# A two-block transformer kernel: tile sizes rounded to 64 bytes, and a pool mixer that leaves PSUM in one VectorE instruction

## The chip, the cores and the metric

The kernel runs on one core of a Trainium2 chip, in fp32. The metric is the device time of one execution in microseconds (us), as the median of three runs.

## The reference, cut to what matters

A first block of two attention layers gives x. It ends in a normalisation by `final_norm_gain`. A second block of one layer follows: a pooling mixer on the normalised x, added to x, and then a convolutional feed-forward network (FFN), added again. All sequences are 1024 long and 1024 wide.

```python
def pool_mixer(x, w, b, scale):              # x: normalised once more
    cs = jnp.pad(jnp.cumsum(xf, axis=1), ((0, 0), (1, 0), (0, 0)))
    for gi, w_len in enumerate((2, 4, 8, 16)):          # four groups of 256 features
        c = cs[..., gi * 256:(gi + 1) * 256]
        lo = jnp.maximum(pos + 1 - w_len, 0)
        window_sum = c[:, 1:] - jnp.take(c, lo, axis=1)
        groups.append(window_sum / count - xf[..., gi * 256:(gi + 1) * 256])
    d = jnp.stack(groups, axis=2)
    y = jnp.einsum('bsgc,gcd->bsgd', d, w).reshape(bsz, seq, 1024) + b
    return scale * y

def conv_ffn(x, w_in, conv_w, conv_b, w_out):           # hidden 2816, conv of 3 taps
    val, gate = jnp.split(causal_depthwise_conv(x @ w_in, conv_w, conv_b), 2, axis=-1)
    return (jax.nn.silu(gate) * val) @ w_out

x = x + pool_mixer(rms_norm(x, norm_mix_g), pool_w, pool_b, pool_scale)
x = x + conv_ffn(rms_norm(x, norm_ffn_g), ffn_w_in, ffn_conv_w, ffn_conv_b, ffn_w_out)
```

## The kernel before

Activations lie feature by feature: 128 features of a tile on the partitions, 512 tokens (a "chunk" c) along the free dimension. A projection in full precision is three matmuls of 128x512 on rounded halves (`mm3`, L257, L260, L261): high weights by high activations, high by low, low by high. For each weight tile `load_w` takes a DMA into a buffer `wraw` (three buffers), a ScalarE rounding into `whi` (L238) and a subtraction into `wlo` (L138) on VectorE or GpSimd. All DMAs are issued from the SyncE queue, in order. The order of the instructions on each engine is drawn up ahead by a scheduler that simulates the program and goes by priorities; on the chip every engine runs its own list in order and waits on semaphores.

The stages that the change touches come last:

- `out1` projects the outputs of the second attention layer with `wo1`. Its operands are eight tiles in `hh`/`hl` and the tiles `yh8` to `yl11` of `y_parts` (eight tiles of 4096 bytes a partition), from a pool allotted at the right-hand end of the memory; a pool `oj` there holds the residual `xr`. Layer 0's projection uses `y_parts` too, but from a pool on the left.
- `pool_chunk(c)` is the normalisation and the mixer of one chunk, once for each half of the tokens. For each of eight feature tiles k it forms the twice normalised activation `h` in VectorE (L1403), scales x in place to the residual (ScalarE by `gf`, L1404, then GpSimd by `bf`, L1405), adds shifted copies for the window sum (L1413), and forms the difference `df` (L1417, L1419, L138). `dense32` then loads the group's weights through the ring `wraw` (`load_f32`), multiplies in fp32 (L313, two instructions per pair of tiles) and leaves PSUM by ScalarE with scale and bias into a tile `pt` (L1429); VectorE adds `pt` to x (L1430), and `norm_split` rounds the result to `hh` (L1178) and `hl` (L1179) for the FFN and sums its squares on GpSimd (L1190).
- Chunk 0 of the mixer is woven with `out1`'s projection of chunk 1; chunk 1 of the mixer is woven with the first six FFN feature tiles of chunk 0 (`FC`).
- `ffn` then alternates blocks of input projections (operands `hh`/`hl`) with blocks of output projections (operands `ah`/`al`, ten tiles of 4096 bytes from the pool `ff`). A convolution buffer `hz` and its carry `ht` come first in that pool.

Tiles of a pool are allotted back to back, each rounded up to 32 bytes a partition. In the program before this gives the following start addresses, by the remainder of a division by 64 bytes. `vecs` (968 bytes, 992 allotted) puts `onesr`, `two` and `bd` at a remainder of 32, and `bd` (8 bytes, 32 allotted) brings the pools behind it back to 0: weights, `hh`, `hl`, `ev`, and nearly all tiles of both attention layers. The right-hand end at which the pools of `out1` begin, counting down, is 229344, a remainder of 32; all tiles of `y_parts` and `xr` there stand at 32. In `ff`, `ht` (352 bytes) puts one of the two `hz` and all of `ah` and `al` at 32.

Of the kernel before, what the change touches and what calls it, by code (L numbers as in the profile page):

```python
# [8 lines left out]
F32 = mybir.dt.float32  # L9
F32R = mybir.dt.float32r  # L10
AF = mybir.ActivationFunctionType
ALU = mybir.AluOpType
# [21 lines left out]
NVEC = _vec_layout()  # L34

GORD = (0, 1, 3, 2)
# [104 lines left out]
class Build:  # L141
# [57 lines left out]
    def setup(self):  # L199
        nc = self.nc  # L200
        c = self.const = self.pool("const", 1)
        self.ident = c.tile([128, 128], F32, name="ident")
        self.dma(out=self.ident, in_=self.A["ident"])
        self.vecs = c.tile([128, NVEC], F32, name="vecs")
        self.dma(out=self.vecs, in_=self.A["vecs"])
        self.onesr = c.tile([128, 128], F32R, name="onesr")
        self.ones = raw(self.onesr)
        nc.gpsimd.memset(self.ones, 1.0)
        two = c.tile([128, 256], F32R, name="two")
        nc.gpsimd.memset(raw(two), 0.0)  # L210
        nc.gpsimd.memset(raw(two[:, 64:192]), 2.0)
        self.twor = two[:, 64:192]
        self.sel = [two[:, 128:256], two[:, 0:128]]
        self.bd = c.tile([128, 2], F32, name="bd")
        nc.gpsimd.memset(self.bd, 0.0)
        nc.gpsimd.memset(self.bd[0:64, 0:1], 1.0)
        nc.gpsimd.memset(self.bd[64:128, 1:2], 1.0)
        self.small = self.pool("small", 2)
        self.wp = self.pool("wp", 4)
        self.mm = self.pool("mm", 2, PSUM)  # L220
# [6 lines left out]
    def load_w(self, src, n, engs=None):  # L227

        nc = self.nc
        res = []  # L230
        for o in range(0, n, 512):
# [3 lines left out]
            for q in range(0, m, 512):  # L235
# [5 lines left out]
                res += [(hi[:, i:i + 128], lo[:, i:i + 128], hi, lo) for i in range(0, e, 128)]  # L241
        return res

    def load_f32(self, src, n):

        res = []
        for o in range(0, n, 512):
            m = min(512, n - o)
            w = self.wp.tile([128, m], F32, tag="wraw", name="w", bufs=self.wp.bufs - 1)
            self.dma(out=w, in_=src[:, o:o + m])  # L250
            res += [w[:, i:i + 128] for i in range(0, m, 128)]
        return res
# [25 lines left out]
    def dense(self, src, rhs, nk, evac, chunks=(0, 1), cw=512, key=None, ps_pool=None, ks=None, engs=None):  # L278
# [26 lines left out]
        return Job(lambda: self.load_w(src, nk * 128, engs), body, key, getattr(self, "done", None))  # L305

    def dense32(self, src, rhs, nk, evac, chunks=(0, 1), ps_pool=None):

        def body(w):
            for c in chunks:  # L310
                ps = (ps_pool or self.mm).tile([128, 512], F32, tag="mm", name="ps")
                for k in range(nk):
                    self.nc.tensor.matmul(ps, w[k], rhs(k, c), start=k == 0, stop=k == nk - 1, skip_group_check=True)  # L313
                self.run_deferred()
                evac(c, ps)
                yield 0.65 * nk
        return Job(lambda: self.load_f32(src, nk * 128), body)

# [997 lines left out]
    def out1(self):  # L1316
# [3 lines left out]
        with ExitStack() as st:  # L1320
            P = lambda n, b, **k: st.enter_context(self.tc.tile_pool(name=n + "n", bufs=b, side="right", **k))
            yp = P("yp", 1)
            oj = P("oj", 2)
# [45 lines left out]
    def pool_chunk(self, c, accf, accm, gfm, psb, invc, tail):  # L1369
# [23 lines left out]
        accz = self.rbc[:, cs]  # L1393
        keep = []
        for g in GORD:
            ds = []
            for kk in range(2):
# [5 lines left out]
                nc.vector.scalar_tensor_tensor(out=h[:, 16:528], in0=x, scalar=gfm[:, k:k + 1], in1=bm, op0=ALU.mult, op1=ALU.mult)  # L1403
                nc.scalar.activation(x, x, AF.Copy, scale=self.v("gf", k))  # L1404
                nc.gpsimd.tensor_tensor(out=x, in0=x, in1=bf, op=ALU.mult)  # L1405
                if c == 0:
                    nc.gpsimd.tensor_copy(tail[:, k, :], h[:, 512:528])
# [14 lines left out]
                yield 1.0  # L1422
            for f in range(2):
                ft = 2 * g + f

                def evac(_, ps, ft=ft):
                    x = X[:, ft, cs]
                    t = oj.tile([128, 512], F32, tag="df", name="pt", bufs=2)
                    nc.scalar.activation(t, ps, AF.Identity, scale=self.v("ps", ft), bias=psb[:, ft:ft + 1])  # L1429
                    nc.vector.tensor_tensor(out=x, in0=x, in1=t, op=ALU.add)  # L1430
                    self.norm_split(x, "gz", ft, self.hh[:, ft, cs], self.hl[:, ft, cs], accz, ft == 2 * GORD[0], keep if ft in GK[7:] else None)
                yield from self.dense32(A["wpl"][ft], lambda k, c: ds[k], 2, evac, (c,), ps_pool=self.px)
        rz = self.rstd([accz] + keep, 4, f"rz{c}", px)
# [4 lines left out]
    def ffn(self, before):  # L1438
# [6 lines left out]
        with ExitStack() as st:  # L1445
            f = st.enter_context(self.tc.tile_pool(name="ff", bufs=2))
            ht = f.tile([128, 44, 2], F32, name="ht", bufs=1)
            nc.gpsimd.memset(ht, 0.0)
# [3 lines left out]
            def conv_evac(j, i, kind):  # L1452
                def evac(c, ps):
                    cs = slice(c * 512, (c + 1) * 512)
                    z = f.tile([128, 514], F32, tag="hz", name="hz", bufs=2)
                    nc.vector.tensor_copy(z[:, 0:2], ht[:, j, :])
# [205 lines left out]
```

## Time and profile before

| | |
|---|---|
| median of 3 runs | 2449.55 us (2443.07 to 2453.1) |
| profiled execution | 2446.46 us, span 2444.7 us |
| mean granted TensorE clock | 0.977 |
| TensorE matmul busy | 2333.7 us, 95% of the span |
| VectorE, ScalarE, GpSimd busy | 1729.5, 1088.9, 925.1 us |

The span runs from the first to the last instruction of the profiled execution. A busy matmul row includes its pipelined end, so the pace of matmuls is read from how many start in a stretch. An engine's idle time counts only where something on the path to the end waits for it. `PEld` is the weight load that goes with each matmul; its count in a stretch is that of the matmuls that begin there.

### The profile page before, as it was taken

The numbers are of one execution on the slowest core, as the hardware profiler recorded it, in microseconds if no ns is written. First come the engines' busy times: TensorE is split into PE (matmuls) and PEld (weight loads), VectorE is DVE, ScalarE is ACT, GpSimd is POOL, SyncE is SP. The second block draws the span as 40 slices with busy tenths as digits, with TensorE's granted clock in tenths as the row PEclk, the third lists the DMA queues.
The fourth block names the chain that finished last, engine by engine and source line by source line (L and its number), as shares of the span: only waits on it lengthen the run. The fifth ranks groups of instructions, "written<-read, shape, count | busy, mean of one in ns | idle before, by whom it ended". The sixth has DMA issues, their size and how long they took to land.

```text
span 2444.7 us, 32782 instructions
## 1 busy us (share of the span) xinstructions
PE 2333.7 (95%) x11118; PEld 1910.1 (78%) x11118; DVE 1729.5 (71%) x2856; ACT 1088.9 (45%) x2037; POOL 925.1 (38%) x773
## 2 busy tenths in 40 slices
PE   7989999989999999999999999999899999999999
PEld 6966777767878878888888887866678888888887
DVE  6767886777895557777887889598977464646554
ACT  5425555565663445434443445444444131323231
POOL 3117887891120235646674762475600000000000
PEclk9989999999999999999999999999899999999999
DMA  6752234234456566776766656422222111111112
GB/s 206 215 147 65 77 106 134 78 108 132 128 197 208 197 198 180 193 199 177 216 170 189 182 177 230 153 88 72 63 80 80 44 52 45 51 48 48 49 47 91
DMA packets 234111, 312.74 MB, mean 128 GB/s; under 512 B 101815, under 2 KB 119671, under 8 KB 233944
## 3 DMA queue, kind: packets, MB, share of 16 engines
q1 hardware_dynamic: 233944, 310.65, 42.1%
q8 instruction: 88, 1.44, 0.2%
q14 instruction: 79, 0.65, 0.1%
HBM read 223.45 MB, written 87.03 MB: 127 GB/s over the span
## 4 chain that ended last, share of the span: by engine, by line
PE 73%; DVE 12%; DMA 4%; issue 4%; POOL 3%; ACT 2%; SPq 0%; DVEq 0%; POOLq 0%; ACTq 0%
PE ps L260 20%; PE ps L257 20%; PE ps L261 20%; DVE wlo L138 2%; PE s L550 2%; PE o L610 2%; PE s L551 2%; PE o L609 2%; POOL acc L599 1%; POOL pl L138 1%; DVE pl L138 1%; PE s L1218 1%; PE s L810 1%; DVE mcg L811 1%; PE pt L915 1%
## 5 line engine op out<-in xcount | busy, mean ns | idle before, releaser
L257 PE MATMUL ps<-hh,whi 128*128 128x512 f32 x1888 | 749.1, 399 | 18.4 <-ACT hh L411 8.5
L260 PE MATMUL ps<-hl,whi 128*128 128x512 f32 x1888 | 751.1, 398 | 8.4 <-DVE hl L412 7.6
L261 PE MATMUL ps<-hh,wlo 128*128 128x512 f32 x1888 | 751.9, 399 | 3.6 <-DVE wlo L138 2.5
L238 ACT CAST whi<-wraw 128x512 fp32r<-128x512 f32 (+1 forms) x400 | 244.9, 615 | 467.8 <-PE ps L260 375.4
L257 PEld LDWEIGHTS ps<-hh,whi 128*128 128x128 f32 x1888 | 361.7, 192 | 97.7 <-ACT hh L411 8.5
L260 PEld LDWEIGHTS ps<-hl,whi 128*128 128x128 f32 x1888 | 361.6, 192 | 87.4 <-DVE hl L412 9.3
L261 PEld LDWEIGHTS ps<-hh,wlo 128*128 128x128 f32 x1888 | 361.2, 191 | 81.7 <-DVE wlo L138 3.7
L599 POOL TENSOR_TENSOR acc<-acc,p 128x512 f32<-128x512 f32 (+2 forms) x272 | 323.8, 1198 | 238.4 <-ACT p L465 177.4
L138 DVE TENSOR_TENSOR wlo<-wraw,whi 128x512 fp32r<-128x512 f32 (+1 forms) x388 | 327.2, 847 | 73.0 <-ACT whi L238 63.9
L138 POOL TENSOR_TENSOR pl<-p,ph 128x384 fp32r<-128x384 f32 (+1 forms) x160 | 200.9, 1258 | 10.6 <-ACT ph L467 8.9
L1485 DVE TENSOR_TENSOR xacc<-ps,xacc 128x512 f32<-128x512 f32 x96 | 66.3, 691 | 131.4 <-PE ps L261 130.9
L1457 DVE TENSOR_TENSOR hz<-ps,rbc 128x512 f32<-128x512 f32 x88 | 60.6, 690 | 117.9 <-PE ps L261 114.1
L467 ACT CAST ph<-p 128x512 fp32r<-128x512 f32 (+1 forms) x240 | 131.5, 560 | 23.2 <-PE d L628 6.0
L260 PE MATMUL ps<-al,whi 128*128 128x512 f32 x352 | 139.1, 396 | 0.0
L261 PE MATMUL ps<-ah,wlo 128*128 128x512 f32 x352 | 138.7, 396 | 0.0
L257 PE MATMUL ps<-ah,whi 128*128 128x512 f32 x352 | 138.4, 396 | 0.0
L610 PE MATMUL o<-pl,V 128*64 128x512 f32 (+3 forms) x368 | 121.1, 348 | 13.8 <-POOL pl L138 7.3
L1461 ACT ACTIVATE cv<-hz,vecs 128x512 f32<-128x512 f32 x88 | 71.6, 816 | 130.7 <-DVE hz L1457 128.0
L609 PE MATMUL o<-ph,V 128*128 128x512 f32 (+3 forms) x368 | 118.6, 340 | 4.0 <-ACT ph L917 3.3
L465 ACT ACTIVATE p<-p 128x384 f32<-128x384 f32 (+2 forms) x128 | 66.6, 524 | 110.3 <-DVE p L1245 109.9
L465 ACT ACTIVATE p<-s 128x512 f32<-128x512 f32 x112 | 66.5, 596 | 80.7 <-PE s L551 47.8
L138 DVE TENSOR_TENSOR pl<-p,ph 128x512 fp32r<-128x512 f32 x80 | 85.1, 1064 | 21.7 <-ACT ph L467 19.3
(256 smaller groups left out, 4439.2 us busy)
## 6 DMA issues: line engine op xcount, KB each, us to landing
wraw<-in_w SPq DMA_DIRECT2D x116, 256.0 KB, 3.5
wraw<-in_wfi SPq DMA_DIRECT2D x112, 256.0 KB, 2.6
wraw<-in_wo SPq DMA_DIRECT2D x72, 256.0 KB, 3.1
g<-evf SPq DMA_DIRECT2D x48, 256.0 KB, 3.9
wraw<-in_wfo SPq DMA_DIRECT2D x40, 256.0 KB, 2.6
sg<-g SPq DMA_DIRECT2D x32, 256.0 KB, 2.7
y<-O SPq DMA_DIRECT2D x14, 512.0 KB
hl<-y SPq DMA_DIRECT2D x14, 512.0 KB, 9.2
```

The source lines that it names most:

```text
L138: out_eng.tensor_tensor(out=out, in0=a, in1=b, op=ALU.subtract)
L238: nc.scalar.copy(hi, raw[:, q:q + e])
L257: i = mm(ps, wh, h, start=first, stop=False, skip_group_check=True)
L260: mm(ps, wh, l, start=False, stop=False, skip_group_check=True)
L261: mm(ps, wl, h, start=False, stop=last, skip_group_check=True)
L465: nc.scalar.activation(p, s, AF.Exp)
L467: nc.scalar.copy(ph, p)
L599: nc.gpsimd.tensor_tensor(out=t, in0=t, in1=p[:, x0 - a:x1 - a], op=ALU.add)
L609: mm(o, V[s][:, j, :], P[0][:, x], start=new, stop=False, skip_group_check=True)
L610: mm(o[0:64], V[s][:, j, 0:64], P[1][:, x], start=False, stop=i == touch[g][-1], skip_group_check=True)
L1461: nc.scalar.activation(t, z[:, 2:514], AF.Identity, scale=self.v("cw2", j), bias=self.v("cb", j))
L1485: nc.vector.tensor_tensor(out=x, in0=ps, in1=x, op=ALU.add)
```

## The change

Five paddings make tile sizes multiples of 64 bytes: `vecs` from 242 to 256 columns, `bd` from 2 to 16, `ht` from 44 to 48 rows, `hz` from 514 to 528 columns, and an unused tile of 32 bytes that is allotted first at the right-hand end. With them `onesr`, `two`, `bd`, the right-hand `y_parts` and `xr`, both `hz` and all `ah` and `al` start at a remainder of 0. What is read and written in them stays as it was.

In the mixer GpSimd multiplies x by `bf` first; then one ScalarE instruction scales it by `gf` and adds the bias `psb`. PSUM is left by one VectorE instruction, x = `ps` times the mixer's scale + x; the tile `pt` and ScalarE's eviction are gone. The mixer's weights get four buffers of their own (`wpl`): four are fetched when a chunk begins, and one more behind each feature tile's matmuls. `load_f32` and `dense32` are removed.

```diff
-        self.vecs = c.tile([128, NVEC], F32, name="vecs")
+        self.vecs = c.tile([128, -(-NVEC // 16) * 16], F32, name="vecs")[:, 0:NVEC]
...
-        self.bd = c.tile([128, 2], F32, name="bd")
+        self.bd = c.tile([128, 16], F32, name="bd")[:, 0:2]
...
+            P("pad", 1).tile([128, 8], F32, name="pad")
             yp = P("yp", 1)
             oj = P("oj", 2)
...
         keep = []
+        wpl = {}
+
+        def fetch(n):
+            for i in GK[len(wpl):n]:
+                wpl[i] = oj.tile([128, 256], F32, tag="wpl", name="wpl", bufs=4)
+                self.dma(out=wpl[i], in_=A["wpl"][i])
+        fetch(4)
         for g in GORD:
...
-                nc.scalar.activation(x, x, AF.Copy, scale=self.v("gf", k))
                 nc.gpsimd.tensor_tensor(out=x, in0=x, in1=bf, op=ALU.mult)
+                nc.scalar.activation(x, x, AF.Identity, scale=self.v("gf", k), bias=psb[:, k:k + 1])
...
-            for f in range(2):
-                ft = 2 * g + f
-
-                def evac(_, ps, ft=ft):
-                    x = X[:, ft, cs]
-                    t = oj.tile([128, 512], F32, tag="df", name="pt", bufs=2)
-                    nc.scalar.activation(t, ps, AF.Identity, scale=self.v("ps", ft), bias=psb[:, ft:ft + 1])
-                    nc.vector.tensor_tensor(out=x, in0=x, in1=t, op=ALU.add)
-                    self.norm_split(x, "gz", ft, self.hh[:, ft, cs], self.hl[:, ft, cs], accz, ft == 2 * GORD[0], keep if ft in GK[7:] else None)
-                yield from self.dense32(A["wpl"][ft], lambda k, c: ds[k], 2, evac, (c,), ps_pool=self.px)
+            for ft in (2 * g, 2 * g + 1):
+                ps = self.px.tile([128, 512], F32, tag="mm", name="ps")
+                for k in range(2):
+                    nc.tensor.matmul(ps, wpl[ft][:, k * 128:(k + 1) * 128], ds[k], start=k == 0, stop=k == 1, skip_group_check=True)
+                fetch(min(len(wpl) + 1, 8))
+                x = X[:, ft, cs]
+                nc.vector.scalar_tensor_tensor(out=x, in0=ps, scalar=self.v("ps", ft), in1=x, op0=ALU.mult, op1=ALU.add)
+                self.norm_split(x, "gz", ft, self.hh[:, ft, cs], self.hl[:, ft, cs], accz, ft == 2 * GORD[0], keep if ft in GK[7:] else None)
+                yield 1.3
...
-            ht = f.tile([128, 44, 2], F32, name="ht", bufs=1)
+            ht = f.tile([128, 48, 2], F32, name="ht", bufs=1)
...
-                    z = f.tile([128, 514], F32, tag="hz", name="hz", bufs=2)
+                    z = f.tile([128, 528], F32, tag="hz", name="hz", bufs=2)
```

## Rows read from the trace of the kernel before

**Rows 1.** The page, busy us of TensorE with share and instructions.
```profile
PE 2333.7 (95%) x11118; PEld 1910.1 (78%) x11118; DVE 1729.5 (71%) x2856; ACT 1088.9 (45%) x2037; POOL 925.1 (38%) x773
```

**Rows 2.** Windows of 20 us: length, busy us (x instructions) by engine, granted clock, DMA.
```profile
1600.00:1620.00 20.00, 19.53 (x74) 13.61 (x73) 19.90 (x27) 9.92 (x16) 15.85 (x16) 1.00 0.25 75
1620.00:1640.00 20.00, 14.79 (x47) 9.70 (x46) 18.83 (x16) 9.57 (x16) 19.19 (x15) 0.83 0.34 105
...
1700.00:1720.00 20.00, 13.21 (x35) 7.43 (x34) 20.00 (x25) 9.40 (x15) 13.27 (x11) 0.80 0.19 56
...
1800.00:1820.00 20.00, 20.00 (x88) 16.17 (x87) 14.43 (x27) 5.48 (x11) 0.00 (x0) 1.00 0.21 63
```

**Rows 3.** Windows over whole FFN blocks: output, output, then input projections.
```profile
1890.41:1935.21 44.80, 44.80 (x193) 36.07 (x192) 19.07 (x29) 6.95 (x12) 0.00 (x0) 1.00 0.17 52
...
2022.28:2067.08 44.80, 44.80 (x194) 36.07 (x192) 19.07 (x29) 6.95 (x12) 0.00 (x0) 1.00 0.17 52
2067.09:2154.14 87.05, 87.05 (x385) 72.06 (x384) 54.72 (x99) 30.96 (x46) 0.00 (x0) 1.00 0.15 46
```

**Rows 4.** Windows of matmuls on y tiles alone: layer 0's, then out1's.
```profile
828.11:844.43 16.32, 16.32 (x73) 13.52 (x72) 10.71 (x13) 11.14 (x12) 2.49 (x2) 1.00 0.46 150
1548.46:1570.87 22.41, 22.41 (x97) 17.98 (x96) 14.33 (x16) 11.53 (x19) 14.54 (x12) 1.00 0.57 189
```

**Rows 5.** One line's instructions over the span: ns min/median/max, first and last start.
```profile
L628 PEld LDWEIGHTS d<-ah,two x48: 187/188/192, 251.7 to 1450.0; 128*128 128x128 f32 x48
```

**Rows 6.** Windows over the mixer's two stretches, columns as in rows 2.
```profile
1590.00:1668.00 78.00, 71.87 (x275) 51.34 (x273) 70.00 (x82) 38.05 (x63) 61.43 (x51) 0.96 0.27 85
1692.00:1783.00 91.00, 77.32 (x278) 54.36 (x276) 88.89 (x108) 45.29 (x73) 55.09 (x39) 0.91 0.22 69
```

**Rows 7.** Groups by line from 1590 to 1800: busy us, mean ns | idle before.
```profile
L1405 POOL TENSOR_TENSOR xacc<-xacc,bf 128x512 f32<-128x512 f32 x16 | 24.3, 1521 | 13.3 <-ACT xacc L1404 13.3
...
L1179 DVE SCALAR_TENSOR_TENSOR hl<-xacc,vecs,hh 128x512 fp32r<-128x512 f32 x16 | 18.9, 1184 | 1.6 <-ACT hh L1178 1.6
...
L1430 DVE TENSOR_TENSOR xacc<-xacc,pt 128x512 f32<-128x512 f32 x16 | 16.5, 1030 | 3.2 <-ACT pt L1429 3.2
...
L1429 ACT ACTIVATE pt<-ps,psb,vecs 128x512 f32<-128x512 f32 x16 | 12.2, 768 | 1.2 <-PE ps L313 1.1
...
L1404 ACT ACTIVATE xacc<-xacc,vecs 128x512 f32<-128x512 f32 x16 | 11.5, 723 | 26.9 <-DVE hx L1403 26.9
```

**Rows 8.** Single lines of VectorE: ns min/median/max; L1457 between 1590 and 1790.
```profile
L1430 DVE TENSOR_TENSOR xacc<-xacc,pt x16: 675/684/1776, 1612.3 to 1774.9; 128x512 f32<-128x512 f32 x16
...
L1457 DVE TENSOR_TENSOR hz<-ps,rbc x14: 676/679/693, 1679.4 to 1789.7; 128x512 f32<-128x512 f32 x14
```

**Rows 9.** TensorE's waits from 1590 to 1800: us in total, times, longest.
```profile
PE ps L313 <- DMA w<-in_wpl: 5.2, 2, 3.8
PE ps L257 <- DVE hz L1457: 5.0, 2, 3.6
PE ps L313 <- DVE df L1417: 4.7, 2, 2.8
PE ps L261 <- DVE wlo L138: 3.0, 3, 2.1
...
PE ps L257 <- ACT whi L238: 1.1, 2, 0.8
```

**Rows 10.** Timeline around the longest wait for mixer weights: start us, us, engine.
```profile
1622.33 0.37 SPq L158 DMA_DIRECT2D w<-in_wpl  x1
...
1624.53 0.17 DVE L138 TENSOR_TENSOR df<-df,hx 128x16 f32<-128x16 f32 x1
...
1624.92 3.75 PE L313 MATMUL ps<-df,w 128*128 128x512 f32 x4 [3.79 <-DMA w<-in_wpl]
```

**Rows 11.** Waits of the SyncE queue from 1580 to 1800, as in rows 9.
```profile
SPq L158 <- DVE wlo L138: 95.3, 32, 7.4
...
SPq L158 <- PE ps L313: 19.0, 9, 9.2
```

More of the change, by code (lines that the diff above doesn't have):

```diff
@@ L241, in load_w @@
                 res += [(hi[:, i:i + 128], lo[:, i:i + 128], hi, lo) for i in range(0, e, 128)]
[L242 to L251, printed above, removed]
         return res
@@ L305, in dense @@
         return Job(lambda: self.load_w(src, nk * 128, engs), body, key, getattr(self, "done", None))
[L307 to L317, printed above, removed]
     def held(self, srcs, rhs, nk, chunks, evacs, pools):
```

## The prediction

> **What bounds the kernel now.** I read the page first, then windows over the last third, then the waits and single lines inside the mixer. The page shows TensorE with matmuls in flight for 95% of the span [rows 1]. That share is an average over two kinds of stage. In the FFN from 1800 us on TensorE is never idle [rows 2, 3], so what a matmul costs there goes straight to the end. [...]
>
> Next I looked for whether the remainder of an address shows. It does in TensorE's pace alone. An FFN output block of 192 matmuls takes 44.80 us, 233.3 ns each, and two blocks shown agree to the last digit; an input block of 384 takes 87.05 us, 226.7 ns each [rows 3]. Form, weights and clock are the same; the moving operand is `ah`/`al` (remainder 32) in one and `hh`/`hl` (remainder 0) in the other. That could still be something else of these tiles, so the y tiles are the better witness: the same lines on the same names, first from the left pool (remainder 0) and later from the right-hand one (remainder 32). They run 72 in 16.32 us, 226.7 ns, and 96 in 22.41 us, 233.4 ns [rows 4].
>
> **The paddings.** The span holds 22 x 8 x 2 x 3 = 1056 matmuls on `ah`/`al`. Each gains 233.33 - 226.69 = 6.64 ns: 7.0 us, all of it at the bound. `out1` has 4 x 8 x 2 x 3 = 192 on the right-hand y tiles at 6.7 ns: 1.3 us, half of them in chunk 0's projection and half in the first mixer stretch. Together 8.3 us; the bounds are 0, if the remainder is not the cause, and 8.3. The weight load of `two` at remainder 32 takes a median of 188 ns [rows 5], and the load beside aligned FFN matmuls 72.06 / 384 = 188 [rows 3], so `onesr`, `two` and `bd` bring nothing. What ScalarE and VectorE write into `ah`, `al` and `hz`, and the `xr` loads, are hidden in the FFN and `out1` behind TensorE; if that cover were gone I see no row that would price them above nothing.
>
> [...]
>
> **Eviction.** Sixteen ScalarE evictions of 0.768 us leave, 12.2 us. ScalarE is half idle in both stretches (38.1 of 78, 45.3 of 91 [rows 6]); I count that at nothing. VectorE's sixteen additions L1430 stay in number and change in kind. They take 675 ns at best and 1776 at worst, 1.030 us in the mean, 16.5 us [rows 7, 8]. The delay falls on instructions with two SBUF inputs while GpSimd is at work: `hl` (L1179) stands at 1.184 in the same stretch [rows 7]. L1457 reads PSUM and one SBUF tile of the same size, in the middle of that traffic, and all fourteen lie between 676 and 693 [rows 8]. The new eviction has those operands, with a scalar from a tile besides. From below it could take 0.68 us without any delay, and if it also left GpSimd alone for as long, up to 16 x 0.684 = 10.9 us of waiting on either side would go. From above it could be delayed like L1179: 16 x 1.184 = 18.9 us, 2.4 lost. I take 0.70 by L1457, its nearest row: 11.2 us, 5.3 us less of VectorE. VectorE is full in one stretch and nearly so in the other, so I count all 5.3.
>
> [...]
>
> **Weights of their own.** TensorE waits twice for `in_wpl`, 5.2 us, once 3.8 [rows 9]. I would gladly take all of it, but the timeline shows what is late next: that load is issued at 1622.33, the matmul starts at 1624.92, and the small subtraction that finishes `df` ends at 1624.53 + 0.17 = 1624.70 [rows 10]. The weights were 0.2 us behind the data. The second wait is at most 5.2 - 3.8 = 1.4. Bounds 0 and 5.2; I take 0.2 + 1.4 = 1.6. SyncE's queue loses its waits for L313 on the ring, 19.0 us, but its large waits are for `wlo`, 95.3 us [rows 11], so the weight loads behind gain nothing while VectorE is late. The new loads 5 to 8 of a chunk, and chunk 1's first four, wait in that queue for an L313 four tiles back; the `wraw` loads of `wo1` and the FFN stand behind them. Those L313 are earlier ones than before, and the waits take the place of nine longer ones: nothing, unless the queue's order puts a fetch too early; nine such waits cost 19.0 us without showing in TensorE's list.
>
> **Residual ahead.** The order was `h`, ScalarE, GpSimd; it becomes `h`, GpSimd, ScalarE: the same two instructions in a row, 0.72 and 1.52 us [rows 7], and x is needed only after a window sum and a matmul. GpSimd stops waiting for ScalarE (13.3 us), but ScalarE, which waited for `h` (26.9 us), now also waits for GpSimd's 1.52 us. Behind it in ScalarE's list stand `whi` roundings and `hh`. Bounds: 13.3 of GpSimd's idle time gained, 16 x 1.52 = 24.3 us lost. ScalarE's slack and a list drawn up for the new order make me take 0.
>
> **The sum.** 8.3 + 5.3 + 1.6 = 15.2 us. The profiled execution took 2446.46 us, 1.8 more than its span, and would take 2431.3. The median of the runs is 3.1 above that execution, so the median to expect is **2434.4 us**, 0.6% below 2449.55.
>
> **Rivals.** *The mixer gives nothing.* VectorE and GpSimd stay as full as they are, or another order of the lists eats the 6.9 us: TensorE's other waits there, `hz` 5.0, `df` 4.7, `wlo` 3.0 [rows 9], all come from VectorE. For it: the stretch ends by VectorE, and the nearest stall moved 0.2 us. Against: the PSUM row is spared every time. Time 2449.55 - 8.3 = 2441.3.
>
> *The paddings give nothing*, since a matmul's pace goes by columns, and something else of those pools or their stages costs the 7 ns. For it: both slow families come from the last pools allotted. Against: the y tiles, and FFN blocks of the two kinds with DMA equally light (0.17 and 0.15) [rows 3]. Time 2449.55 - 6.9 = 2442.7. [...]
>
> *ScalarE stuck behind GpSimd (slower).* In program order a residual scaling that waits for GpSimd's multiplication holds up the next `whi`, then `wlo`, then the matmul and the `wraw` ring. For it: waits for `whi` already end TensorE's idle time twice (1.1 us) [rows 9], and GpSimd is at 61.4 of 78. Against: ScalarE idles for half. If every scaling is exposed by one multiplication the loss is 24.3 us and the time 2449.55 - 15.2 + 24.3 = 2458.7; if a further GpSimd instruction of that length lies ahead in each case, 48.6 us and 2483.0. Slower than before it becomes from 15.2 us, 0.95 per scaling, and measurably so from 27.5, 1.7 per scaling.
>
> **How the numbers follow.** Half a per cent, 12.2 us, is about what a measurement of this kernel can tell from no change: faster means below 2437.3, slower above 2461.8. The forecast gets 0.52; the mixer giving nothing 0.25; the paddings giving nothing 0.08; both nothing 0.03; ScalarE behind GpSimd 0.12, of which 0.05 lie above 2461.8. The forecast's own range is 2425 to 2438: downwards by the other ends, 10.9 for 5.3 and 5.2 for 1.6, upwards by the 3 us between runs. Faster: nearly all of the forecast, and 0.03 of the first rival, when it moves a little, 0.55. Slower 0.05, same 0.40. The range reaches up over the first two rivals to 2446; the third and "both nothing" are largely left out, with some of the second.
>
> **What would show it.** Right: output blocks of the FFN at 43.5 us for 192, the later y stretch at 21.8 for 96; the new eviction at 0.68 to 0.75 us in all sixteen; no wait of L313 for `wpl`; the two mixer stretches together shorter by 5 to 9 us with VectorE still full. Wrong: blocks still at 44.8 us (the remainder is not the cause); evictions at 1.1 us or more; ScalarE waiting for x of GpSimd and TensorE for `whi`; a longer stretch before 1800 in which another wait of VectorE takes over. The prediction fails upwards most easily in the mixer, whose order of instructions I can't see.

## The result, and the profile after

The changed kernel takes 2434.38 us, median of five runs (2429.21 to 2435.2), against 2449.26 for the kernel before on the same chip: 0.9941, with a 95% interval of 0.9921 to 0.9960, 14.9 us less. The forecast was 2434.4. The number was met; most of what follows says that two of its terms came out as they did for reasons other than the ones given.

The page of the changed kernel, TensorE's line, answers to [rows 1]:

```profile
PE 2319.2 (95%) x11118; PEld 1905.2 (78%) x11118; DVE 1720.1 (71%) x2856; ACT 1079.2 (44%) x2021; POOL 921.8 (38%) x773
```

The same number of matmuls keeps TensorE busy 14.5 us less. To see where, I cut both traces at two landmarks which the change leaves alone: the first matmul on the later y tiles, and the first matmul of the FFN on `ah`. Windows of the kernel before, from landmark to landmark and from there to the end (columns as in [rows 2]: length, busy us of TensorE, weight load, VectorE, ScalarE and GpSimd with instructions, granted clock, DMA share, GB/s):

```profile
1548.46:1802.70 254.24, 230.78 (x921) 172.39 (x920) 212.00 (x275) 125.81 (x207) 150.84 (x115) 0.93 0.28 88
1802.70:2444.70 642.00, 638.38 (x2785) 522.53 (x2783) 360.25 (x617) 182.68 (x273) 1.30 (x1) 1.00 0.18 57
```

The changed kernel, in order of time: the later y stretch, the window from landmark to landmark, the two mixer stretches, the window from there to the end, and an output block and an input block of the FFN ([rows 4], [rows 6], [rows 3]):

```profile
1547.28:1569.68 22.40, 22.40 (x98) 17.99 (x97) 13.38 (x16) 11.55 (x19) 14.56 (x12) 1.00 0.64 214
1547.28:1794.46 247.18, 222.98 (x921) 168.31 (x920) 201.83 (x275) 116.20 (x191) 148.91 (x115) 0.97 0.28 90
1590.00:1668.00 78.00, 71.35 (x276) 51.58 (x275) 69.10 (x85) 35.26 (x58) 63.57 (x55) 0.96 0.29 90
1692.00:1783.00 91.00, 73.44 (x281) 51.94 (x280) 88.05 (x115) 42.13 (x68) 52.09 (x38) 0.96 0.18 60
1794.46:2431.90 637.44, 633.91 (x2785) 522.45 (x2783) 360.21 (x617) 182.72 (x273) 1.29 (x1) 1.00 0.18 57
1881.78:1925.74 43.96, 43.96 (x193) 36.06 (x192) 19.07 (x29) 6.95 (x12) 0.00 (x0) 1.00 0.17 53
...
1925.74:2012.84 87.10, 87.10 (x386) 72.07 (x385) 54.72 (x99) 30.99 (x46) 0.00 (x0) 1.00 0.15 46
```

Three things are to be seen.

*The FFN* is 642.00 - 637.44 = 4.6 us shorter. An output block of 192 went from 44.80 to 43.96 us, 233.3 to 229.0 ns a matmul; 226.7 was forecast.

*The later y stretch* still takes 22.40 us for 96, 233.3 ns, although its tiles now start at a multiple of 64 bytes. The remainder, which the prediction took for the cause, is gone, and the pace has not moved.

*The mixer*, from the y stretch to the FFN, is 254.24 - 247.18 = 7.1 us shorter, where 6.9 was forecast and some of the 1.3 of the y tiles besides. But not because TensorE waits less. The same 921 matmul records are busy for 230.78 us before and 222.98 after, 7.8 us less; what is left as idle time went from 23.5 to 24.2. The granted clock rose from 0.93 to 0.97 of full speed. The times within this window at which the clock stood at its lower level, 0.50 of full speed, come to these sums, first before, then after:

```profile
sum 34.13, PE 26.73 PEld 18.43 DVE 32.26 ACT 16.22 POOL 24.07; mean PE 5.35 PEld 3.69 DVE 6.45 ACT 3.24 POOL 4.81
sum 17.07, PE 11.94 PEld 8.11 DVE 15.51 ACT 7.29 POOL 10.03; mean PE 3.98 PEld 2.70 DVE 5.17 ACT 2.43 POOL 3.34
```

TensorE was busy at the lower level for 26.73 us before and 11.94 after. In the kernel before, matmuls of 128x512 start 0.43 us apart at the lower level (1628.89 to 1629.75) and 0.23 at the upper (from 1630.58 on). By these two paces about half of the difference, 7.4 us, is what the same work saves at the upper level, an estimate, and that is nearly all of the 7.8. So the gain lies in matmuls that ran at the full clock instead of 0.50 of it, and the windows of the two stretches say where: the second, 0.91 before, is at 0.96; the first is at 0.96 in both.

TensorE's largest waits in the changed kernel from 1590 to 1795 (us in total, times, longest), to be laid beside [rows 9]:

```profile
PE ps L247 <- DVE hz L1441: 5.9, 1, 5.9
PE ps L1412 <- issue: 5.8, 1, 5.8
PE ps L247 <- DVE hz L1442: 4.6, 3, 2.2
PE ps L1412 <- DVE df L1403: 3.9, 3, 1.9
PE ps L247 <- ACT hh L1156: 1.1, 1, 1.1
```

The waits for the mixer's weights are gone, and one wait for `hz` (5.9 us, where the longest was 3.6) and one ahead of a matmul of the mixer (5.8) are longer. The second bears "issue", that is, no releaser that the profile could name; VectorE's timeline ahead of that matmul (it starts at 1628.37) names it:

```profile
1620.44 1.65 DVE L1157 SCALAR_TENSOR_TENSOR hl<-xacc,vecs,hh 128x512 fp32r<-128x512 f32 x1 [1.24 <-ACT hh L1156]
1622.01 1.75 DVE L1403 SCALAR_TENSOR_TENSOR df<-sx,hx 128x512 f32<-128x512 f32 x1
1623.69 1.75 DVE L1157 SCALAR_TENSOR_TENSOR hl<-xacc,vecs,hh 128x512 fp32r<-128x512 f32 x1
1625.36 1.55 DVE L138 TENSOR_TENSOR wlo<-wraw,whi 128x512 fp32r<-128x512 f32 x1
1626.83 1.23 DVE L1405 TENSOR_TENSOR df<-sx,invc 128x16 f32<-128x16 f32 x1
1628.10 0.17 DVE L138 TENSOR_TENSOR df<-df,hx 128x16 f32<-128x16 f32 x1
```

`df` is finished at 1628.27, 0.1 us before the matmul. Ahead of it `hl` and `wlo`, which that matmul does not need, stand in VectorE's list, each at more than twice its best time in this trace (0.737 and 0.670 us).

Lines of the changed kernel from 1590 to 1800 (busy us, mean ns | idle before), answering to [rows 7]:

```profile
L1390 POOL TENSOR_TENSOR xacc<-xacc,bf 128x512 f32<-128x512 f32 x16 | 27.3, 1707 | 9.2 <-DVE hx L1389 9.2
L1157 DVE SCALAR_TENSOR_TENSOR hl<-xacc,vecs,hh 128x512 fp32r<-128x512 f32 x16 | 20.1, 1254 | 1.8 <-ACT hh L1156 1.7
L1391 ACT ACTIVATE xacc<-xacc,psb,vecs 128x512 f32<-128x512 f32 x16 | 13.0, 814 | 27.9 <-POOL xacc L1390 27.9
```

The new eviction alone (ns min/median/max), answering to [rows 8]:

```profile
L1415 DVE SCALAR_TENSOR_TENSOR xacc<-ps,vecs,xacc x16: 735/740/751, 1609.4 to 1770.4; 128x512 f32<-128x512 f32 x16
```

All sixteen evictions escape the delay: 0.735 to 0.751 us, against 1.030 in the mean before. But other instructions take longer: `hl` went from 1.184 to 1.254 us, GpSimd's multiplication from 1.521 to 1.707. ScalarE now waits 27.9 us for that multiplication; none of TensorE's waits is put down to the scaled x.

### The profile page after: what moved, and what is told of

Its sections match the earlier page's. It is cut to its first block, busy times and chain, and to the rows that moved or that the text cites. A ratio compares the mean times of both kernels' runs of the same rounds, so it can differ in the third digit from the quotient of the medians.

```text
span 2431.9 us, 32762 instructions
## 1 busy us (share of the span) xinstructions
PE 2319.2 (95%) x11118; PEld 1905.2 (78%) x11118; DVE 1720.1 (71%) x2856; ACT 1079.2 (44%) x2021; POOL 921.8 (38%) x773
## 4 chain that ended last, share of the span: by engine, by line
PE 77%; DVE 11%; DMA 3%; issue 3%; ACT 2%; POOL 2%; SPq 0%; DVEq 0%; ACTq 0%; POOLq 0%
PE ps L247 21%; PE ps L250 21%; PE ps L251 21%; PE s L528 2%; DVE wlo L138 2%; PE o L588 2%; PE s L529 2%; PE o L587 2%; POOL acc L577 1%; PE s L788 1%; DVE pl L138 1%; DVE mcg L789 1%; PE s L1196 1%; PE pt L893 1%; POOL pl L138 1%
## 5 line engine op out<-in xcount | busy, mean ns | idle before, releaser
L138 DVE TENSOR_TENSOR wlo<-wraw,whi 128x512 fp32r<-128x512 f32 (+1 forms) x388 | 322.0, 834 | 77.2 <-ACT whi L238 67.2
L1442 DVE TENSOR_TENSOR hz<-ps,rbc 128x512 f32<-128x512 f32 x88 | 60.6, 690 | 117.2 <-PE ps L251 114.3
L445 ACT CAST ph<-p 128x512 fp32r<-128x512 f32 (+1 forms) x240 | 131.6, 560 | 23.3 <-PE o L587 6.1
```

The costliest lines, as they stand in the source:

```text
L138: out_eng.tensor_tensor(out=out, in0=a, in1=b, op=ALU.subtract)
L445: nc.scalar.copy(ph, p)
```

## The experiments

They fall in two families: what sets a matmul's pace, and what the parts of the mixer are worth. Times are given as ratios to the kernel before on the same chip, with the differences in us that follow from them. What the parts of the mixer are worth is read from windows between the two landmarks, in one profiled execution of each kernel. In the new mixer these windows repeat closely where the instructions are the same: 247.18 in the changed kernel, 247.15 and 247.18 in two of the kernels below. In the old mixer, as the first experiment shows, they differ by 2.9 us with the same instructions in the same order, so a difference of that size between two windows proves little by itself.

### The paddings alone, the mixer alone

The kernel before with the five paddings:

```diff
...
+            P("pad", 1).tile([128, 8], F32, name="pad")
...
-            ht = f.tile([128, 44, 2], F32, name="ht", bufs=1)
+            ht = f.tile([128, 48, 2], F32, name="ht", bufs=1)
...
```

> The kernel before with the five paddings alone. The forecast's theory (a start at a multiple of 64 bytes brings a matmul to 226.7 ns): 8.3 us off, FFN output blocks of 192 at 43.5 us and the later y stretch of 96 at 21.8. What the changed kernel's trace already showed would repeat as 43.96 us per block, 4.6 us off in the FFN, nothing for the y tiles: about 2444.7. The rival that the paddings give nothing: 2449.3, and then the 4.6 us of the FFN come from the mixer's rewrite.

And the changed kernel without them:

```diff
...
-            P("pad", 1).tile([128, 8], F32, name="pad")
...
-            ht = f.tile([128, 48, 2], F32, name="ht", bufs=1)
+            ht = f.tile([128, 44, 2], F32, name="ht", bufs=1)
...
```

> The changed kernel without the five paddings: the mixer's rewrite alone. If the two halves add up, 7 us off (the changed trace is 7.06 us shorter from the later y stretch to the FFN), about 2442.3, with FFN output blocks back at 44.80 us. If the mixer gives nothing by itself, 2449.3. If the paddings bring all and more through the mixer's tiles, less than 3 us off.

The paddings alone: 0.9962 [0.9949, 0.9976], 9.3 us less. The mixer alone: 0.9971 [0.9956, 0.9985], 7.1 us less. Windows of the paddings alone: the y stretch, landmark to landmark, the FFN:

```profile
1551.81:1574.20 22.39, 22.39 (x97) 18.01 (x96) 13.47 (x16) 11.53 (x19) 14.55 (x11) 1.00 0.59 190
1551.81:1803.13 251.32, 227.28 (x921) 170.37 (x920) 209.44 (x275) 126.10 (x207) 152.36 (x115) 0.95 0.28 89
1803.13:2440.60 637.47, 633.91 (x2785) 522.62 (x2783) 359.99 (x617) 182.74 (x273) 1.29 (x1) 1.00 0.18 57
```

The sums of its times at the lower clock level between the landmarks:

```profile
sum 27.31, PE 20.95 PEld 13.31 DVE 25.27 ACT 15.19 POOL 18.96; mean PE 4.19 PEld 2.66 DVE 5.05 ACT 3.04 POOL 3.79
```

Windows of the mixer alone: landmark to landmark, the FFN:

```profile
1546.71:1793.86 247.15, 222.69 (x921) 168.18 (x920) 204.34 (x275) 116.10 (x191) 148.85 (x115) 0.97 0.29 90
1793.86:2435.90 642.04, 638.38 (x2785) 522.53 (x2783) 360.11 (x617) 182.75 (x273) 1.30 (x1) 1.00 0.18 57
```

In the FFN the split is clean: 637.5 with the paddings, 642.0 without. In the mixer it is not: the rewrite alone gives the whole 7.1 us, and the paddings, put into the old mixer, 2.9. Those 2.9 are no pace of the y tiles (22.39 us), and no other list either: the two traces show the same instructions in the same order on TensorE, VectorE and ScalarE. TensorE was idle for 24.0 us against 23.5, and busy for 3.5 less. At the lower clock level it was busy for 20.95 us against 26.73, and half of that difference is 2.9. So with unchanged lists the clock alone moved the old mixer by 2.9 us. Whether the addresses or the chance of one execution did it, no run shows.

### Distance from the weights, not remainder

The addresses that the compiled programs give suggested a reading of the FFN and the y tiles: what the slow and the fast families differ in is the distance between the start of the moving operand (the activations) and the start of the weights, modulo 512 bytes. It is 0 for `hh`, `hl` and the early y tiles; before, it is -32 for `ah`/`al` and +32 for the later y tiles; after, +64 and -64. So two paddings were enlarged to make both 0:

```diff
-            P("pad", 1).tile([128, 8], F32, name="pad")
+            P("pad", 1).tile([128, 120], F32, name="pad")
...
-            ht = f.tile([128, 48, 2], F32, name="ht", bufs=1)
+            ht = f.tile([128, 104, 2], F32, name="ht", bufs=1)
```

> The changed kernel with two paddings enlarged, so that ah, al and the later y tiles start at the same address as the weights modulo 512 bytes, not 64 bytes beyond or short of it. Theory of the difference (a matmul's pace goes by how far the start of the moving operand lies from that of the weights, modulo 512 bytes): output blocks of 192 at 43.5 us, the later y stretch of 96 at 21.8, 2.4 + 1.3 = 3.7 us less than the changed kernel, 2430.7. Theory of the remainder by 64: all are at remainder 0 already, nothing changes, blocks 43.96, y 22.4, 2434.4. Theory that something else of those stages costs it (copies, transfers): as the remainder, nothing.

Measured: 2428.52 us, 0.9921 [0.9902, 0.9940], 19.3 us less than before. Windows: the y stretch, landmark to landmark, the FFN, an output block, an input block:

```profile
1546.12:1567.90 21.78, 21.78 (x97) 17.96 (x96) 13.33 (x16) 11.44 (x19) 14.14 (x11) 1.00 0.68 222
1546.12:1792.25 246.13, 222.46 (x922) 169.14 (x920) 202.00 (x275) 115.88 (x191) 149.31 (x115) 0.96 0.29 91
1792.25:2427.00 634.75, 631.20 (x2785) 522.33 (x2783) 360.05 (x617) 182.76 (x273) 1.29 (x1) 1.00 0.18 57
1879.29:1922.81 43.52, 43.52 (x194) 36.04 (x192) 19.06 (x29) 6.95 (x12) 0.00 (x0) 1.00 0.18 55
1922.81:2009.85 87.04, 87.04 (x386) 72.07 (x384) 54.73 (x99) 31.00 (x46) 0.00 (x0) 1.00 0.15 46
```

Both slow families reach the pace of the fast ones: 43.52 us for 192 and 21.78 for 96, 226.7 and 226.9 ns. Every start was a multiple of 64 bytes in the changed kernel already, so the remainder cannot have done it, and TensorE's list of instructions is the changed kernel's to the last one.

The counter-test moves the weights, `hh`, `hl`, `ah`, `al` and the early y tiles together to remainder 32:

```diff
+        c.tile([128, 8], F32, name="shift")
         self.small = self.pool("small", 2)
```

> The changed kernel with a tile of 32 bytes put ahead of the weights, so that the weights, hh, hl, ah, al and the first y tiles all start at remainder 32 by 64, with their distances from each other as they were; only the later y tiles stay where they are. Theory of the remainder: all 5664 matmuls on hh and hl go to 233.3 ns, 6.6 ns each, 37 us more, FFN input blocks of 384 at 89.6 us, about 2472. Theory of the difference: input blocks stay at 87.1 and output blocks at 43.96, time as the changed kernel within 2 us, about 2434.4.

Measured: 0.9961 [0.9944, 0.9978], 2436.98 us. Windows: the y stretch, landmark to landmark, output block, input block:

```profile
1553.44:1575.93 22.49, 22.49 (x98) 18.06 (x97) 13.47 (x16) 11.60 (x20) 14.59 (x12) 1.00 0.66 214
1553.44:1800.62 247.18, 222.87 (x921) 168.35 (x920) 201.91 (x275) 116.09 (x191) 148.85 (x115) 0.97 0.29 90
...
1887.94:1931.90 43.96, 43.96 (x193) 36.06 (x192) 19.06 (x29) 6.95 (x12) 0.00 (x0) 1.00 0.17 53
1931.90:2018.99 87.09, 87.09 (x385) 72.10 (x384) 54.70 (x99) 30.97 (x46) 0.00 (x0) 1.00 0.16 46
```

All at remainder 32, and the pace of the blocks is the changed kernel's: 43.96 and 87.09 against 43.96 and 87.10. The remainder costs these matmuls nothing. The later y tiles, now at -96 from the weights, take 22.49 us for 96, 234.3 ns.

The last of the three puts `hh` and `hl` 64 bytes away from the weights; `ah` and `al`, allotted behind them, move along to +128:

```diff
+        self.hp.tile([128, 16], F32, name="shift")
         self.hh = self.hp.tile([128, 8, S], F32R, name="hh")
```

> The changed kernel with a tile of 64 bytes put ahead of hh and hl alone: they start 64 bytes beyond the weights modulo 512 instead of level with them; every start stays at remainder 0 by 64. Theory of the difference: FFN input blocks of 384 go from 87.1 us to 87.9 (229.0 ns, as ah and al at +64 had it), all 5664 matmuls on hh and hl cost 2.3 ns more, 13 us, about 2447; ah and al move to +128, which no run has shown. Theory of the remainder by 64, or of the stage: input blocks at 87.1, time 2434.4.

Measured: 2447.9 us, 1.0005 [0.9992, 1.0017]: 64 bytes of padding, at a multiple of 64, give back the whole gain of the change. Windows: an output block, an input block:

```profile
1892.64:1937.27 44.63, 44.63 (x194) 36.18 (x193) 19.07 (x29) 6.94 (x12) 0.00 (x0) 1.00 0.17 52
1937.27:2025.18 87.91, 87.91 (x386) 72.12 (x385) 54.80 (x99) 30.91 (x46) 0.00 (x0) 1.00 0.16 46
```

The input block goes to 87.91 us, 228.9 ns, as `ah` and `al` had it at +64; the forecast by distance was 87.9 and 2447. At +128 `ah`/`al` take 232.4 ns.

A scan was meant to give the period and the shape, with one distance for each buffer of `ah` and `al`:

```diff
-f.tile([128, S], F32R, tag="a" + n, name="a" + n, bufs=5)
+f.tile([128, S + 16], F32R, tag="a" + n, name="a" + n, bufs=5)[:, 0:S]
```

> The changed kernel with ah's and al's five buffers spaced 64 bytes further apart, so that they start at +64, +128, +192, +256, +320 (ah) and +384, +448, 0, +64, +128 (al) from the weights modulo 512; all at remainder 0 by 64. Theory of the difference: single matmuls of one block differ by buffer, 226.7 ns for the one at 0 and 229 to 235 for the others; if the period is 256 bytes, +256 also stands at 226.7. Theory of the remainder: all alike.

One profile, 2436.12 us. An output block and an input block:

```profile
1882.14:1926.63 44.49, 44.49 (x194) 36.02 (x192) 19.08 (x29) 6.94 (x12) 0.00 (x0) 1.00 0.17 53
1926.63:2013.71 87.08, 87.08 (x385) 72.10 (x384) 54.73 (x99) 30.98 (x46) 0.00 (x0) 1.00 0.15 46
```

The output block stands at 231.7 ns in the mean, the input block as ever. By single matmuls, as means of 64 to 66 distances from one start to the next, `ah` on the rounded weights takes 229.9, 233.0, 230.2, 233.4 and 230.6 ns at +64, +128, +192, +256 and +320. So +256 is not like 0: the period is not 256 bytes. But `al` at 0 takes 229.7 where 226.7 was expected. Its neighbours in that block lie at other distances, and what a matmul costs may hang on the one beside it, which no run shows; the shape of the effect stays open. What is shown is that equal starts modulo 512 are the fast case and that every other distance tried was slower by 2 to 8 ns in whole blocks.

### The parts of the mixer, singly

Eviction alone: the kernel before with the paddings, without the mixer's bias, and

```diff
-                    t = oj.tile([128, 512], F32, tag="df", name="pt", bufs=2)
-                    nc.scalar.activation(t, ps, AF.Identity, scale=self.v("ps", ft), bias=psb[:, ft:ft + 1])
-                    nc.vector.tensor_tensor(out=x, in0=x, in1=t, op=ALU.add)
+                    nc.vector.scalar_tensor_tensor(out=x, in0=ps, scalar=self.v("ps", ft), in1=x, op0=ALU.mult, op1=ALU.add)
```

> The kernel before with the paddings and the eviction by VectorE alone; the weights come by the old ring, the residual is scaled in the old order, and the bias psb is left out. Forecast's term: 5.3 us less than the paddings alone (2439.0), 2433.7, sixteen evictions at 0.68 to 0.75 us, and the time from the later y stretch to the FFN 251.3 - 5.3 = 246.0. Rival, the gain of the mixer lies in the weights or the order: no change from the paddings alone, 251.3 and 2439.0.

The weights put back into the ring, in the changed kernel:

```diff
-                    nc.tensor.matmul(ps, wpl[ft][:, k * 128:(k + 1) * 128], ds[k], start=k == 0, stop=k == 1, skip_group_check=True)
-                fetch(min(len(wpl) + 1, 8))
...
+                yield from self.dense32(A["wpl"][ft], lambda k, c: ds[k], 2, evac, (c,), ps_pool=self.px)
```

> The changed kernel with the mixer's weights back in the shared ring, eviction and order as changed. Forecast's term: 1.6 us more than the changed kernel, the time from the later y stretch to the FFN 247.2 + 1.6 = 248.8, TensorE waiting for the weights' load again. Rivals: none, 247.2, what is late next takes the place of the weights; or the whole 5.2 us, 252.4, because VectorE is no longer 0.2 us behind the load.

The old order of the residual in the changed kernel, without the mixer's bias:

```diff
-                nc.gpsimd.tensor_tensor(out=x, in0=x, in1=bf, op=ALU.mult)
-                nc.scalar.activation(x, x, AF.Identity, scale=self.v("gf", k), bias=psb[:, k:k + 1])
+                nc.scalar.activation(x, x, AF.Copy, scale=self.v("gf", k))
+                nc.gpsimd.tensor_tensor(out=x, in0=x, in1=bf, op=ALU.mult)
```

> The changed kernel with the residual scaled in the old order (ScalarE first, then GpSimd), eviction and weights as changed; the bias psb is left out. Forecast's term: 0, 247.2 us from the later y stretch to the FFN. Rivals: the new order brought part of GpSimd's 13.3 us of waiting, so the old one costs up to that, 249 to 260; or the new order held ScalarE up behind GpSimd and the old one is faster, 240 to 246.

Weights alone, in the kernel before with the paddings:

```diff
...
+                wpl[i] = oj.tile([128, 256], F32, tag="wpl", name="wpl", bufs=2)
...
+        fetch(2)
...
-                    t = oj.tile([128, 512], F32, tag="df", name="pt", bufs=2)
+                t = oj.tile([128, 512], F32, tag="pt", name="pt", bufs=1)
```

> The kernel before with the paddings and weights in tiles of their own alone, in a ring of two tiles, since four do not fit beside the old eviction's tile; that tile has one buffer instead of two; eviction by ScalarE and the order are the old ones. Theory that the weights carry the mixer's gain, by ending the stalls of TensorE after which the clock was low: 247 to 249 us from the later y stretch to the FFN, against 251.3 with the paddings alone. Theory that they do so only with VectorE's eviction beside them: 251 to 254.

The new order alone, in the kernel before with the paddings:

```diff
-                nc.scalar.activation(x, x, AF.Copy, scale=self.v("gf", k))
                 nc.gpsimd.tensor_tensor(out=x, in0=x, in1=bf, op=ALU.mult)
+                nc.scalar.activation(x, x, AF.Identity, scale=self.v("gf", k), bias=psb[:, k:k + 1])
...
-                    nc.scalar.activation(t, ps, AF.Identity, scale=self.v("ps", ft), bias=psb[:, ft:ft + 1])
+                    nc.scalar.activation(t, ps, AF.Copy, scale=self.v("ps", ft))
```

> The kernel before with the paddings and the new order of the residual alone (GpSimd first, then ScalarE with the bias; the eviction without the bias). If each part has a worth of its own, what the order cost when it was undone (2.5 us) is lost here too: 253.8 us from the later y stretch to the FFN against 251.3. If the parts are worth only what the stalls happen to do, no sign can be told, 248 to 254.

The windows from landmark to landmark, in this order, one of each kernel. Eviction alone, 0.9975 [0.9965, 0.9986]:

```profile
1548.92:1803.02 254.10, 229.01 (x921) 172.40 (x920) 201.31 (x275) 114.74 (x191) 146.68 (x115) 0.93 0.27 88
```

Ring again, 0.9966 [0.9952, 0.9979]:

```profile
1546.73:1797.97 251.24, 227.93 (x921) 171.75 (x920) 202.67 (x275) 115.59 (x191) 148.99 (x115) 0.95 0.28 89
```

Old order again, 0.9947 [0.9932, 0.9962]:

```profile
1545.10:1789.82 244.72, 222.80 (x922) 167.97 (x920) 202.31 (x275) 114.71 (x191) 148.41 (x115) 0.97 0.29 91
```

Weights alone, 0.9977 [0.9965, 0.9990]:

```profile
1543.75:1800.57 256.82, 229.98 (x922) 172.14 (x920) 212.22 (x275) 125.09 (x207) 150.96 (x115) 0.93 0.27 87
```

New order alone, 0.9963 [0.9950, 0.9976]:

```profile
1548.16:1798.68 250.52, 224.66 (x921) 167.81 (x920) 206.62 (x275) 125.56 (x207) 152.85 (x115) 0.97 0.28 89
```

*Eviction.* The evictions take 0.740 us each, and VectorE is busy 209.44 - 201.31 = 8.1 us less than with the paddings alone, more than the 5.3 forecast. The stretch does not follow: 254.1, where 246.0 was forecast and the paddings alone take 251.3, the clock at 0.93 against 0.95. The rival (nothing from the eviction) is the nearer of the two, and the ratios agree: 0.9975, no faster than the 0.9962 of the paddings alone.

*Weights.* Put back into the ring they cost 251.24 - 247.18 = 4.1 us, where 1.6 was forecast and 5.2 was the upper bound. TensorE's list is another one here too. The idle time is hardly other (23.3 against 24.2): TensorE is busy 4.95 us longer, at 0.95 of the clock. The waits for the load are back, in the trace of the ring kernel as its largest single sum:

```profile
PE ps L313 <- DMA w<-in_wpl: 6.4, 3, 3.8
PE ps L257 <- DVE hz L1454: 6.2, 2, 4.8
PE ps L261 <- DVE wlo L138: 4.6, 3, 3.1
```

In the old mixer, in a ring of two, own weights make it worse: 256.8 against 251.3. That kernel also has one buffer of its own for the evicted tile instead of two shared ones, so it says little of the weights by themselves.

*Order.* Back to the old one the stretch is 2.5 us shorter, 244.72, with TensorE's list unchanged; TensorE's idle time fell from 24.2 to 21.9. So in this one execution the new order costs something; the ratios, 0.9947 [0.9932, 0.9962] and 0.9941 [0.9921, 0.9960], don't tell the two apart. It has the sign of the rival with ScalarE behind GpSimd and a tenth of its 24.3 us; that ScalarE's waiting is the cause is not shown, since ScalarE's own list changed in other places too. In the old mixer the new order gains 0.8 us, too little to be told from nothing. Laid beside the paddings alone (251.3) the parts make +2.8, +5.5 and -0.8 us one by one, and -4.1 together: they can't be added up.

### Filling a stall

To ask whether the clock alone sets the mixer's time, six spare matmuls were put ahead of the matmul at 1628.37, on top of the enlarged paddings:

```diff
+                for _ in range(6 if (c, ft) == (0, 6) else 0):
+                    nc.tensor.matmul(ps, self.ident, bm, start=True, stop=True, skip_group_check=True)
```

> The changed kernel with both enlarged paddings, and six spare matmuls of f32 (0.86 us each, 5.1 in all) on bm, whose result is overwritten, ahead of the one matmul of chunk 0 before which TensorE stood for 5.8 us. Theory that the mixer's time is the clock's: the stretch of half clock behind that stall (6.8 us, 3.4 lost) goes, 243 us from the later y stretch to the FFN against 246.1 without the spare matmuls, 2425. Theory that VectorE sets it: 246.1 or up to 1 us more, since nothing of VectorE's is earlier.

Measured: 2439.34 us, 0.9976 [0.9960, 0.9991], slower than without them. Its window from landmark to landmark:

```profile
1554.05:1809.96 255.91, 232.44 (x933) 173.37 (x932) 195.82 (x275) 116.13 (x191) 150.60 (x115) 0.95 0.28 87
```

TensorE's timeline at the spare matmuls and at the matmul that they were meant for (start us, us):

```profile
1615.76 3.60 PE L1412 MATMUL ps<-bm,ident 128*128 128x512 f32 x8
...
1620.91 1.45 PE L1412 MATMUL ps<-bm,ident 128*128 128x512 f32 x3
...
1630.56 2.92 PE L1414 MATMUL ps<-df,wpl 128*128 128x512 f32 x4 [2.75 <-DVE df L138]
```

The planner put them where their inputs were ready, some 8 us ahead of that matmul, and drew up another list besides (each spare matmul is two records; the view ends before the last one). They did not fill the stall, and the stretch is 9.8 us longer than with the enlarged paddings alone (246.13). VectorE was busy for only 195.82 us, the least of all kernels, in the second longest of the stretches. The question that this run was made for is not answered by it.

## Why the prediction was right, and where not

**The paddings, 8.3 us.** The step that failed is the cause, "whether the remainder of an address shows", and with it the size. Before, `ah`/`al` and the later y tiles happened to be both at remainder 32 and at a distance of 32 bytes from the weights modulo 512, and the tiles at remainder 0 were at distance 0: the rows of before could not tell the two apart, and the y tiles, taken for the better witness, had the same double mark. The padding moved the distances from -32 to +64, which is a little faster, and from +32 to -64, which is not. The FFN's 7.0 measured 4.6, the y tiles' 1.3 measured 0. With the distances at 0 both terms come out as forecast: the FFN 642.00 - 634.75 = 7.2, the y stretch 0.6 for its first half.

A matmul's columns alone do not give its time in these runs: 226.7, 229.0, 232.4, 233.3 and 234.3 ns stand beside each other for the same 512 columns, with the operands' distance as the one thing varied in three of the kernels.

**The eviction, 5.3 us.** Its duration was nearly right, 0.740 for 0.70. The remaining 0.04 goes with the form: `hx` (L1389), the same operation with SBUF inputs alone, has a best of 737 ns, and `hz` (L1442), a plain multiplication of two tensors with one input from PSUM, a best of 675 ns. The step that failed is "VectorE is full in one stretch and nearly so in the other, so I count all 5.3". Alone it bought VectorE 8.1 us and the stretch nothing. At the 5.8 us stall shown above, what TensorE waits for is `df`, and `hl` and `wlo` stand ahead of it: there the order in VectorE's list counts, not the sum of its work. That the other stalls are of this kind is not shown.

**Weights of their own, 1.6 us.** Too small: 4.1 in the one execution, inside the bounds. The waits themselves bought nothing: the two for the load (5.2 us) stood ahead of the fourth and the fifth of the chunk's eight outputs, and in the changed kernel the fifth waits 5.8 us for `df`. What was not counted is the matmuls at the lower clock level: with the ring the window stands at 0.95 of the clock against 0.97, and TensorE was busy 4.95 us longer for the same matmuls, and idle no longer.

**The residual ahead, 0.** It costs 2.5 us in the changed kernel by the one trace and nothing that the ratios show, within the bounds. ScalarE waits 27.9 us for GpSimd, and no wait of TensorE's is put down to that, as the forecast had it.

**The sum.** 6.9 for the mixer measured 7.1 by the trace, but the terms inside are not the ones that make it: the idle time did not shrink at all, and the busy time of the same matmuls shrank by 7.8. Trace and medians differ too: by the landmarks the change brings 4.6 + 7.1 = 11.7 us and 1.2 ahead of them, 12.8 of span, against 14.9 [9.8, 19.4] between the medians. By the trace the 15.2 us of the sum are missed by 3.5, about what the paddings fell short by (2.4 in the FFN, 1.3 in the y tiles). And ahead of the first landmark, where all kernels go through the same instructions in the same order, the profiled executions of those with `hh` and `hl` at distance 0 lie 10 us apart (1543.75 to 1554.05). That the median fell on the forecast to the digit is luck.

**Among the rivals**, "the paddings give nothing" is refuted in the FFN and right for the y tiles; of its ground, that a matmul's pace goes by columns, the trace of before shows 119.9 ns for 256 columns (75 matmuls, 900.41 to 909.28) beside 226.7 for 512, and the runs show 226.7 to 234.3 for 512 alone. "ScalarE stuck behind GpSimd" comes to 2.5 us at most. "The mixer gives nothing" is refuted in its time, 7.1 us, though what spoke for it holds: VectorE is still busy for 88.05 of 91 us in the second stretch.

What stays open: why just this combination of the three parts loses 0.03 of the stretch to the low clock where the old mixer lost 0.07. The planner redraws the lists with every edit of the mixer, and each run of a part is also a run of another list. That the clock, and not the idle time, carries the difference is read from the windows. The paddings alone come nearest to an experiment that holds the lists and changes the clock, 2.9 us; what moved the clock there is open as well.

The fastest version of all is the changed kernel with the two enlarged paddings, 0.9921 [0.9902, 0.9940].

## What to carry to other kernels

When two families of matmuls with the same shape run at different paces, write down the start of the moving operand and of the weights and compare them modulo 512 bytes before padding anything; a padding to a round number can help, do nothing, or cost some 13 us in this kernel. Where an engine looks full, ask which instruction in its list TensorE waits for, since time saved elsewhere in the list need not reach it. And in a stretch with stalls compare busy time, idle time and granted clock of TensorE separately: a gain can sit wholly in the clock. Before a few us of one window are put down to an edit, compare two executions with the same lists.

## What the runs showed of the hardware

A matmul of 512 columns with weights of 128 by 128 takes 226.7 ns with moving operand and weights at equal starts modulo 512 bytes, 229.0 at +64, 232.4 at +128, 233.3 at -32 and -64, 233.4 at +32, 234.3 at -96. These are means over stretches of 96 to 384 matmuls, at a granted clock of 1.00; at 0.50 such matmuls started 0.43 us apart. Distances of 0 and +64 give the same paces at remainder 32 as at 0.

VectorE's operation with a scalar from a tile and one input from PSUM takes 735 to 751 ns for 128x512, sixteen times in the middle of GpSimd's work, where `hl`, with two SBUF inputs, takes 1254 in the mean. There a multiplication of only 16 columns took 1.23 us, and the subtraction of the same size behind it 0.17.

In the kernel before, `cv` (L1462, SBUF inputs alone) takes 742 to 755 ns from 1810 to 2400 us, where GpSimd is busy for 1.30 us of 590, and 994 in the mean from 1590 to 1800, where it is busy for 127.02 us of 210. The delay is not one of two inputs alone: the copy into `ht` (L1459, one SBUF input) takes 159 to 170 ns in the first of these stretches and 565 in the mean in the second.
